# Pooled products, gate sums and convolution steps in a two-block kernel: where they are issued and on which engine

## The chip, the cores and the metric

The kernel runs on one core of one Trainium2 chip. A core has TensorE (matmul), VectorE, ScalarE and GpSimd, each with an in-order queue of its own, and SyncE, whose queue (SP) issues nearly all transfers here. The metric is the time of one execution on the device in microseconds (us).

## The reference

A first block (attention of two kinds, 32 routed experts, a gated embedding) is followed by a second block of two layers, on 256 rows of 1024 columns. The change touches only the second block, which is, cut to what matters:

```python
for l in range(2):
    mod = silu(c) @ w_ada[l] + b_ada[l]
    shift, scale, gate = split(mod, 3)
    h = rms_norm(x, g_pre[l]) * (1 + scale) + shift
    proj = h @ w_in[l]                    # parts 0 to 5, 512 columns each
    u_a, b_a, c_a, gate_a, u_p, gate_p = parts(proj)
    y_a = b_a * causal_conv3(c_a * u_a, w_conv[l]) * silu(gate_a)
    y_p = pool(u_p, w_pool[l]) * pool_scale[l] * silu(gate_p)
    y = concat(y_a, y_p) @ w_out[l]
    x = x + gate * rms_norm(y, g_post[l])
```

`pool` takes, in four groups of 128 columns, the mean of the last 2, 4, 8 or 16 rows less the row itself, and multiplies each group with its own 128 x 128 matrix. All arithmetic is of float32 accuracy.

## The kernel before

Float32 matmuls of large matrices are made of three passes (`mm3`): each operand is split into an upper half (`hi`, rounded) and a residue (`lo`), and hi x hi, hi x lo and lo x hi are summed in PSUM. For every piece of weights ScalarE makes `hi` (L162), and VectorE or GpSimd makes `lo` = raw - hi (L167). A piece is 512 KB: five raw buffers and six hi/lo pairs rotate. PSUM gives three banks to `bulk` (the projections), four to `bank` (transposes, small products) and one to `spare`.

A layer `l` of the second block runs as follows. `normed` (L1084) makes the normalised rows: GpSimd computes the root, VectorE scales (L1094), TensorE transposes (L1024), ScalarE and VectorE apply scale and shift. The parts are then projected by `project` (L1157), each in two halves of 256 columns: a half is 48 matmuls into two `bulk` banks, which the caller empties. First come part 3 and the first half of part 5, by rows (L1137 to L1148), with the weights that `gates_of` has loaded; then, in this order:

- part 4 (`u_p`): ScalarE copies it into PU; GpSimd adds up the windows (L1184), and PW, the pooled features, gets its main part from VectorE (L1187) and its first 16 columns from GpSimd (L1186, L1188).
- part 5, second half: sigmoid on ScalarE, product on VectorE (L1196).
- the four pooled products (L1197 to L1205): TensorE multiplies PW[j] with the pool matrix into a `bank`; ScalarE or VectorE scales it, `gate` transposes and multiplies the gates (j below 2), `split` makes hi and residue (`Yh`, `Yl`).
- part 0 (`u_a`): ScalarE copies it into CU (L1208).
- `ada_acc` for the third part of `mod` (`gate`): silu(c) times 1024 x 1024 weights, 512 columns per call, summed over eight blocks of 128 rows with the partitions kept apart. With GpSimd as its engine each 512 KB load holds four row blocks of 256 columns: two products, then three additions (L581 to L586). With VectorE each load holds two row blocks of 512 columns: two operations (L576, L578). Loads go to the three buffers `adr`, two of which hold weights of the row gates for part of the time; the sums go to the two `acc` buffers, which the gating products `PP` of the block before use first.
- part 2 (`c_a`): VectorE multiplies it into CU (L1214), which empties the bank, and runs the three convolution steps (L1215 to L1217).
- part 1 (`b_a`): VectorE multiplies it into Y (L1219), then `gate` (L1155) and `split`.

After that the partition sums of `gate` are formed on TensorE, and the output projection and the residual close the layer.

The order of the queues is not written out: the program is traced line by line, and a planner simulates the engines and gives each free engine the ready instruction that was traced first. `tc.issue_after(i)` puts those instructions of its block that run on the engine of `i` behind `i`; those on other engines it leaves free. `roots` holds the GpSimd instructions that end each root. The order found is then fixed, and each engine runs its own queue in order.

Of the kernel before, what the change touches and what calls it, by code (L numbers as in the profile page):

```python
# [15 lines left out]
OP = mybir.AluOpType  # L16
AX = mybir.AxisListType.X

S, D, P = 256, 1024, 128
# [78 lines left out]
def block_kernel(ctx: ExitStack, tc: tile.TileContext, a, out, dbg=None, ne=NE):  # L98
    nc = tc.nc
# [6 lines left out]
    def bank():  # L106
        return psum.tile([P, 512], F32, name="bank", tag="bank", bufs=4)

    def bulk():
        return psum.tile([P, 512], F32, name="bulk", tag="bulk", bufs=3)  # L110

    def spare():
        return psum.tile([P, 512], F32, name="spare", tag="spare", bufs=1)

    def slot(tag, n=2048, dt=F32):
        return phase["pool"].tile([P, n], dt, name=tag, tag=tag, bufs=1)
# [16 lines left out]
    def ada_slot(dt=F32):  # L133
        if early.get("adr"):
            return early["adr"].pop(0)
        return phase["pool"].tile([P, 1024], dt, name="adr", tag="adr", bufs=3)

    def mid(shape, dt=F32):
        return work.tile(shape, dt, name="mid", tag="mid", bufs=8)
# [11 lines left out]
    def mm(o, l, r, start, stop):  # L151
        nc.tensor.matmul(o, l, r, start=start, stop=stop)  # L152

    def mm3(o, l, r, start, stop):

        mm(o, l[0], r[0], start, False)
        mm(o, l[0], r[1], False, False)
        mm(o, l[1], r[0], False, stop)

    def split(raw, dst, eng=None):  # L160

        nc.scalar.copy(dst[0], raw)  # L162
        n = raw.shape[-1]
        w = n if eng is None or len(raw.shape) > 2 else min(n, 512)
        for c0 in range(0, n, w):
            cs = slice(c0, min(n, c0 + w))
            (eng or nc.vector).tensor_sub(dst[1][..., cs], raw[..., cs], dst[0][..., cs].bitcast(F32))  # L167
# [38 lines left out]
    def load_split(src, cn, order=None, room=(), eng=None, gains=None, later=None, raws=None):  # L206


        nk = src.shape[0] // P
        kn = min(nk, 1024 // cn)  # L210
        parts, room = {}, dict(room)
        for i in order or range(nk // kn):
            k0 = i * kn
            raw = ((raws or {}).get(i, raw_slot)())[:, :kn * cn]
            nc.sync.dma_start(raw.rearrange("p (k n) -> p k n", k=kn),
                              src[k0 * P:(k0 + kn) * P].rearrange("(k p) n -> p k n", p=P))
            dst = [v[:, :kn * cn] for v in pair(room.get(i))]
            if gains:
                g = vc(gains, i)
                nc.scalar.activation(dst[0], raw, AF.Copy, scale=g)  # L220
                later.append((nc.vector.scalar_tensor_tensor, dst[1], raw, g, dst[0].bitcast(F32), OP.mult, OP.subtract))
            else:
                split(raw, dst, eng[i] if isinstance(eng, list) else eng)
            parts[i] = [v.rearrange("p (k n) -> p k n", k=kn) for v in dst]
        return lambda k, c0, c1: tuple(v[:, k % kn, c0:c1] for v in parts[k // kn])
# [20 lines left out]
    def vc(name, k=0, n=1):  # L246
        return VC[:, VCOL[name] + k:VCOL[name] + k + n]
# [306 lines left out]
    def ada_acc(l, c, e):  # L554

        acc = work.tile([P, 512], F32, name="acc", tag="acc", bufs=2)
        n = 256 if e is nc.gpsimd else 512
        kn = 1024 // n
        for o in range(0, 512, n):
            v = acc[:, o:o + n]  # L560
            for i in range(0, KD, kn):
                w = ada_slot().rearrange("p (k n) -> p k n", k=kn)
                nc.sync.dma_start(w, a["w_ada_2"][l][i * P:(i + kn) * P, c * 512 + o:c * 512 + o + n]
                                  .rearrange("(k p) n -> p k n", p=P))
                if e is nc.scalar:
                    for k in range(2):
                        e.activation(w[:, k], w[:, k], AF.Copy, scale=cact[:, i + k:i + k + 1])
                    if i:
                        nc.gpsimd.tensor_add(w[:, 0], w[:, 0], w[:, 1])
                        nc.gpsimd.tensor_add(v, v, w[:, 0])  # L570
                    else:
                        nc.gpsimd.tensor_add(v, w[:, 0], w[:, 1])
                elif e is nc.vector:
                    for k in range(kn):
                        if i + k == 0:
                            e.tensor_scalar(v, w[:, 0], cact[:, 0:1], None, op0=OP.mult)  # L576
                        else:
                            e.scalar_tensor_tensor(v, w[:, k], cact[:, i + k:i + k + 1], v, op0=OP.mult, op1=OP.add)  # L578
                else:
                    for k in (0, 2):  # L580
                        e.tensor_mul(w[:, k:k + 2], w[:, k:k + 2],  # L581
                                     cact[:, i + k:i + k + 2].unsqueeze(2).to_broadcast([P, 2, n]))
                    e.tensor_add(w[:, 0:2], w[:, 0:2], w[:, 2:4])  # L583
                    e.tensor_add(w[:, 0], w[:, 0], w[:, 1])
                    if i:
                        e.tensor_add(v, first[:, 0], w[:, 0])  # L586
                    first = w
        return acc
# [371 lines left out]
    for e in range(ne):  # L960
# [6 lines left out]
        if e == max(ne - 2, 0):  # L967
            PP = [[perm.tile([P, 512], F32, name="PP", tag=n) for n in ("TA", "TB")],
                  [work.tile([P, 512], F32, name="PP", tag="acc", bufs=2) for _ in range(2)]]
            for t in range(NT):  # L970
                for h in range(2):
                    po = spare()
# [134 lines left out]
    for t in range(NT):  # L1107
# [14 lines left out]
        for h in range(2):  # L1122
            hs, po = slice(h * 512, (h + 1) * 512), pos[h]
# [9 lines left out]
    for l in range(2):  # L1133
# [4 lines left out]
        for t in range(NT):  # L1138
            for dst, ws in ((G[:, t], wgs[:2]), (GP[:, t], wgs[2:])):
                n = 256 * len(ws)  # L1140
                po, sg = bulk()[:, :n], mid([P, n])
# [8 lines left out]
        def gate(dst, g, j):  # L1150

            pt = bank()[:, :S]
            for t in range(NT):
                nc.tensor.transpose(pt[:, t * P:(t + 1) * P], g[:, t, j * P:(j + 1) * P], ident)
            nc.vector.tensor_mul(dst, dst, pt)  # L1155

        def project(part, js=(0, 2), first=None):  # L1157
            for j in js:
                c0 = part * 512 + j * P
                w = first if first and j == js[0] else load_split(wi[:, c0:c0 + 256], 256)  # L1160
                pos = [bulk() for _ in range(2)]
                for k in range(KD):
                    for i in range(2):
                        mm3(pos[i][:, :S], w(k, i * P, (i + 1) * P), (hm[0][:, k], hm[1][:, k]), k == 0, k == KD - 1)
                for i in range(2):
                    yield j + i, pos[i][:, :S]

        def wcv(i, j):
            return vc("w_conv_2", l * 12 + i * 4 + j)

        PUW = wide(s_pu, F32)
        PU = PUW[:, :4 * (16 + S)].rearrange("p (j n) -> p j n", j=4)
# [16 lines left out]
        Y = slot(s_y).rearrange("p (k n) -> p k n", k=KD)  # L1189
# [3 lines left out]
        for j, po in project(5, (2,)):  # L1193
            sgs.append(small([P, S]))
            nc.scalar.activation(sgs[-1], po, AF.Sigmoid)
            nc.vector.tensor_mul(sgs[-1], sgs[-1], po)  # L1196
        for j in range(4):  # L1197
            px, y = bank(), Y[:, 4 + j]
            mm(px[:, :S], wp[:, l, j * P:(j + 1) * P], PW[:, j], True, True)
            if j < 2:  # L1200
                nc.scalar.activation(y, px[:, :S], AF.Copy, scale=vc("pool_scale_2", l * 4 + j))
                gate(y, GP, j)
            else:
                nc.vector.scalar_tensor_tensor(y, px[:, :S], vc("pool_scale_2", l * 4 + j), sgs[j - 2], op0=OP.mult, op1=OP.mult)
            split(y, (Yh[:, 4 + j], Yl[:, 4 + j]))  # L1205
        CU = PU[:, :, 16:]
        for j, po in project(0):
            nc.scalar.copy(CU[:, j], po)  # L1208
        post = slot(s_post).rearrange("p (i n) -> p i n", i=2)
        nc.sync.dma_start(post, a["post"][l:l + 1].to_broadcast([P, 2, D]))  # L1210
        with tc.issue_after(roots[2 * l + 1]):
            accs = [ada_acc(l, 4 + h, nc.gpsimd) for h in range(2)]
        for j, po in project(2):
            nc.vector.tensor_mul(CU[:, j], CU[:, j], po)  # L1214
            nc.vector.tensor_scalar(Y[:, j], CU[:, j], wcv(2, j), None, op0=OP.mult)  # L1215
            nc.vector.scalar_tensor_tensor(Y[:, j, 1:], CU[:, j, :S - 1], wcv(1, j), Y[:, j, 1:], op0=OP.mult, op1=OP.add)
            nc.vector.scalar_tensor_tensor(Y[:, j, 2:], CU[:, j, :S - 2], wcv(0, j), Y[:, j, 2:], op0=OP.mult, op1=OP.add)  # L1217
        for j, po in project(1):
            nc.vector.tensor_mul(Y[:, j], Y[:, j], po)  # L1219
            gate(Y[:, j], G, j)  # L1220
# [77 lines left out]
```

## Time and profile before

| | |
|---|---|
| median of 3 runs | 1435.12 us (1434.74 to 1435.84) |
| profiled execution: time | 1435.64 us |
| profiled execution: span | 1433.8 us |
| mean granted clock of TensorE, share of full speed | 0.974 |
| busy: TensorE | 1306.5 us (91%) |
| busy: VectorE | 626.0 us (44%) |
| busy: ScalarE | 351.6 us (25%) |
| busy: GpSimd | 321.0 us (22%) |

PE stands for TensorE's matmuls, PEld for its weight loads, DVE for VectorE, ACT for ScalarE, POOL for GpSimd, SP for SyncE. The span runs from the first instruction to the last; the time of an execution is somewhat more. A releaser, behind `<-`, is the instruction or transfer that ended an idle time. A granted clock of 1.00 is 2.4 GHz. Layer 0 of the second block lies at about 1213 to 1325 us of the span, with the change's lines from 1225 to 1300; layer 1 follows to the end.

### The profile page before, as it was taken

What the parts mean: (1) busy time and instruction counts of PE and PEld (TensorE: products, weight loads), DVE (VectorE), ACT (ScalarE), POOL (GpSimd) and SP (SyncE); (2) the same over time, 40 slices, a digit from 0 to 9 for tenths busy, and PEclk for the clock granted to TensorE, in tenths of its full rate; (3) what the DMA queues carried; (4) which work ended last, traced back from release to release, by engine and by line L of the source; (5) the groups of instructions that cost most, each with busy time, mean ns of one, the idle gap of its engine ahead of it and who ended that gap; (6) DMA issues with size and microseconds to landing.
All of it is one profiled execution on the core that took longest, in us unless ns stands there. A gap on an engine that the chain in (4) does not pass through costs nothing. (4 is left out here: it accounts for less than half of the span.)

```text
span 1433.8 us, 17081 instructions
## 1 busy us (share of the span) xinstructions
PE 1306.5 (91%) x6831; PEld 706.2 (49%) x6831; DVE 626.0 (44%) x1005; ACT 351.6 (25%) x630; POOL 321.0 (22%) x353
## 2 busy tenths in 40 slices
PE   7989998999999989989989998998999968899987
PEld 6788884333333332333323333333333337887986
DVE  4899963232232221222313233132121248688685
ACT  6756531111111101011100111011111145435432
POOL 5595471000000000000000000000000035785682
PEclk9999997999999999999999999999999979999999
DMA  9739779999999999999999999999999955756651
GB/s 333 245 119 310 253 277 370 428 428 427 426 429 428 428 428 426 428 429 427 428 426 429 426 429 428 427 427 428 427 428 425 423 200 168 235 179 203 215 182 45
DMA packets 100546, 502.44 MB, mean 350 GB/s; under 512 B 7216, under 2 KB 60720, under 8 KB 75632
## 3 DMA queue, kind: packets, MB, share of 16 engines
q1 hardware_dynamic: 99904, 500.59, 86.8%
q8 instruction: 55, 0.90, 0.3%
q10 hardware_dynamic: 560, 0.73, 0.2%
q14 instruction: 27, 0.22, 0.0%
HBM read 500.24 MB, written 1.05 MB: 350 GB/s over the span
## 5 line engine op out<-in xcount | busy, mean ns | idle before, releaser
L152 PE MATMUL bank<-raw,mid 128*64 128x512 f32 x3072 | 692.5, 603 | 43.7 <-DMA raw<-in_w_gate_up_dram 37.6
L152 PEld LDWEIGHTS bank<-raw,mid 128*64 128x64 f32 x3072 | 213.5, 138 | 484.2 <-issue 399.0
L918 POOL CAST BIAS<-BIAS 128x128 fp32r<-128x128 f32 x32 | 10.3, 324 | 827.6 <-PE bank L152 827.5
L854 DVE TENSOR_SCALAR mid<-bank 128x512 f32<-128x512 f32 x32 | 22.1, 692 | 392.8 <-PE bank L152 392.8
L879 DVE SCALAR_TENSOR_TENSOR Y<-bank,ws,Y 64x512 fp32r<-64x512 f32 x64 | 48.0, 750 | 250.3 <-ACT Y L878 250.3
L856 ACT ACTIVATE mid<-mid 128x512 f32<-128x512 f32 x32 | 20.2, 631 | 436.3 <-DVE mid L854 436.3
L167 DVE TENSOR_TENSOR lo<-raw,hi 128x1024 fp32r<-128x1024 f32 (+2 forms) x91 | 116.5, 1301 | 20.4 <-ACT hi L162 20.2
L162 ACT CAST hi<-raw 128x1024 fp32r<-128x1024 f32 (+1 forms) x102 | 105.8, 1041 | 72.4 <-PE bulk L152 55.7
L878 ACT ACTIVATE Y<-bank,ws 64x512 fp32r<-64x512 f32 x64 | 43.7, 682 | 280.2 <-PE bank L152 254.1
L167 POOL TENSOR_TENSOR lo<-raw,hi 128x512 fp32r<-128x512 f32 x50 | 72.8, 1483 | 39.3 <-ACT hi L162 29.9
L152 PE MATMUL bulk<-XS,OH 128*64 128x512 f32 x256 | 63.2, 614 | 4.7 <-DVE X L891 3.2
L152 PE MATMUL bulk<-hi,s 128*128 128x256 f32 (+2 forms) x256 | 59.7, 325 | 8.0 <-ACT hi L162 7.5
L152 PE MATMUL bulk<-s,hi 128*128 128x256 f32 x320 | 62.8, 293 | 0.0
L578 DVE SCALAR_TENSOR_TENSOR acc<-adr,cact,acc 128x512 f32<-128x512 f32 x49 | 54.2, 1105 | 0.6 <-DMA adr<-in_w_ada_dram 0.2
L581 POOL TENSOR_TENSOR adr<-adr,cact 128x512 f32<-128x512 f32 x32 | 45.1, 1434 | 33.5 <-DMA adr<-in_w_ada_dram 33.5
L152 PEld LDWEIGHTS bulk<-s,hi 128*128 128x128 f32 x320 | 51.1, 195 | 0.7 <-DVE s L608 0.2
L152 PEld LDWEIGHTS bulk<-hi,s 128*128 128x128 f32 x256 | 44.2, 196 | 11.7 <-ACT hi L162 7.5
L152 PE MATMUL bulk<-sc,hi 128*128 128x256 f32 x144 | 42.9, 298 | 3.9 <-DVE se L1219 2.1
L152 PE MATMUL bulk<-sa,hi 128*128 128x256 f32 x144 | 42.9, 298 | 3.8 <-DVE sb L1219 2.1
L152 PE MATMUL bulk<-s,lo 128*128 128x256 f32 x160 | 45.9, 291 | 0.0
L891 DVE TENSOR_TENSOR X<-X,bulk 128x512 f32<-128x512 f32 x64 | 42.3, 682 | 1.1 <-PE bulk L152 0.7
L152 PE MATMUL bulk<-lo,s 128*128 128x256 f32 (+2 forms) x128 | 41.7, 327 | 0.9 <-DVE lo L167 0.9
(447 smaller groups left out, 1932.1 us busy)
## 6 DMA issues: line engine op xcount, KB each, us to landing
raw<-in_w_gate_up_dram SPq DMA_DIRECT2D x128, 2048.0 KB, 31.0
raw<-in_w_down_dram SPq DMA_DIRECT2D x64, 2048.0 KB, 34.6
raw<-in_w_in_dram SPq DMA_DIRECT2D x75, 512.0 KB, 4.9
adr<-in_w_ada_dram SPq DMA_DIRECT2D x48, 512.0 KB, 4.5
raw<-in_w_out_dram SPq DMA_DIRECT2D x23, 512.0 KB, 3.6
raw<-in_w_ple_gate_dram SPq DMA_DIRECT2D x5, 512.0 KB, 5.4
raw<-in_w_branch_b_dram SPq DMA_DIRECT2D x4, 512.0 KB, 7.2
raw<-in_w_branch_a_dram SPq DMA_DIRECT2D x4, 512.0 KB, 5.1
```

Of the source, the lines that this page charges most:

```text
L152: nc.tensor.matmul(o, l, r, start=start, stop=stop)
L162: nc.scalar.copy(dst[0], raw)
L167: (eng or nc.vector).tensor_sub(dst[1][..., cs], raw[..., cs], dst[0][..., cs].bitcast(F32))
L578: e.scalar_tensor_tensor(v, w[:, k], cact[:, i + k:i + k + 1], v, op0=OP.mult, op1=OP.add)
L581: e.tensor_mul(w[:, k:k + 2], w[:, k:k + 2], cact[:, i + k:i + k + 2].unsqueeze(2).to_broadcast([P, 2, n]))
L854: nc.vector.tensor_scalar(g_, pG, 7.0, None, op0=OP.min)
L856: nc.scalar.activation(sg, g_, AF.Sigmoid, scale=1.702)
L878: nc.scalar.activation(Y[sl, 0, h], py[sl], AF.Copy, scale=ws[sl, h:h + 1])
L879: nc.vector.scalar_tensor_tensor(Y[sl, 1, h], py[sl], ws[sl, h:h + 1], Y[sl, 0, h].bitcast(F32), op0=OP.mult, op1=OP.subtract)
L891: nc.vector.tensor_add(xv, xv, pc)
L918: nc.gpsimd.tensor_copy(bs, ONE[:, e, :, None].bitcast(F32).to_broadcast([P, 2, SL]))
```

## The change

Three things. The pooled products are traced behind part 0, and `issue_after` puts the matmuls and transposes of products 0 and 1 behind the last matmul of part 0's first half, those of products 2 and 3 behind that of its second half. `ada_acc` of the gates is called with VectorE in place of GpSimd. In part 2 both banks of a half are multiplied into CU before the convolution steps of the half.

```diff
--- before.py
+++ after.py
@@ -1194,7 +1194,13 @@
             sgs.append(small([P, S]))
             nc.scalar.activation(sgs[-1], po, AF.Sigmoid)
             nc.vector.tensor_mul(sgs[-1], sgs[-1], po)
-        for j in range(4):
+        CU, behind = PU[:, :, 16:], []
+        for j, po in project(0):
+            behind.append(nc.cur_bb.bb.instructions[-1])
+            nc.scalar.copy(CU[:, j], po)
+
+        def pooled(j):
+
             px, y = bank(), Y[:, 4 + j]
             mm(px[:, :S], wp[:, l, j * P:(j + 1) * P], PW[:, j], True, True)
             if j < 2:
@@ -1203,18 +1209,22 @@
             else:
                 nc.vector.scalar_tensor_tensor(y, px[:, :S], vc("pool_scale_2", l * 4 + j), sgs[j - 2], op0=OP.mult, op1=OP.mult)
             split(y, (Yh[:, 4 + j], Yl[:, 4 + j]))
-        CU = PU[:, :, 16:]
-        for j, po in project(0):
-            nc.scalar.copy(CU[:, j], po)
+
+        for j in range(4):
+            with tc.issue_after(behind[0 if j < 2 else 2]):
+                pooled(j)
         post = slot(s_post).rearrange("p (i n) -> p i n", i=2)
         nc.sync.dma_start(post, a["post"][l:l + 1].to_broadcast([P, 2, D]))
         with tc.issue_after(roots[2 * l + 1]):
-            accs = [ada_acc(l, 4 + h, nc.gpsimd) for h in range(2)]
-        for j, po in project(2):
-            nc.vector.tensor_mul(CU[:, j], CU[:, j], po)
-            nc.vector.tensor_scalar(Y[:, j], CU[:, j], wcv(2, j), None, op0=OP.mult)
-            nc.vector.scalar_tensor_tensor(Y[:, j, 1:], CU[:, j, :S - 1], wcv(1, j), Y[:, j, 1:], op0=OP.mult, op1=OP.add)
-            nc.vector.scalar_tensor_tensor(Y[:, j, 2:], CU[:, j, :S - 2], wcv(0, j), Y[:, j, 2:], op0=OP.mult, op1=OP.add)
+            accs = [ada_acc(l, 4 + h, nc.vector) for h in range(2)]
+        gen = project(2)
+        for two in zip(gen, gen):
+            for j, po in two:
+                nc.vector.tensor_mul(CU[:, j], CU[:, j], po)
+            for j, _ in two:
+                nc.vector.tensor_scalar(Y[:, j], CU[:, j], wcv(2, j), None, op0=OP.mult)
+                nc.vector.scalar_tensor_tensor(Y[:, j, 1:], CU[:, j, :S - 1], wcv(1, j), Y[:, j, 1:], op0=OP.mult, op1=OP.add)
+                nc.vector.scalar_tensor_tensor(Y[:, j, 2:], CU[:, j, :S - 2], wcv(0, j), Y[:, j, 2:], op0=OP.mult, op1=OP.add)
         for j, po in project(1):
             nc.vector.tensor_mul(Y[:, j], Y[:, j], po)
             gate(Y[:, j], G, j)
```

## Rows read from the trace of the kernel before

**Rows 1.** By stretch: us, busy PE, PEld, DVE, ACT, POOL, clock, DMA share, GB/s.

```profile
1225.30:1242.20 16.90, 16.90 (x144) 16.90 (x143) 9.53 (x9) 7.84 (x13) 16.07 (x16) 1.00 0.63 204
1242.20:1262.80 20.60, 15.69 (x109) 14.74 (x107) 14.86 (x17) 7.70 (x15) 20.42 (x22) 0.92 0.65 211
1262.80:1293.10 30.30, 27.25 (x209) 26.67 (x208) 28.93 (x36) 11.02 (x15) 20.90 (x15) 0.94 0.56 186
```

**Rows 2.** Waits, 1213 to 1325 us: who for whom, total, times, longest.

```profile
ACT hi L162 <- PE bulk L152: 25.3, 13, 5.3
POOL adr L581 <- DMA adr<-in_w_ada_dram: 16.6, 3, 11.3
DVE sa L1187 <- POOL mid L1184: 8.8, 4, 2.8
...
PE bank L152 <- POOL sa L1188: 4.1, 2, 3.0
...
PE bulk L152 <- DVE se L1219: 2.1, 1, 2.1
...
PE bulk L152 <- DVE sa L1214: 0.9, 1, 0.9
...
PE bulk L152 <- DVE small L1196: 0.8, 1, 0.8
```

**Rows 3.** Timeline of TensorE: start, length, ..., idle time before in brackets.

```profile
1244.13 0.70 PE L152 MATMUL bank<-sa,XS 128*128 128x256 f32 x2 [1.13 <-POOL sa L1188]
...
1254.96 0.70 PE L152 MATMUL bank<-sa,XS 128*128 128x256 f32 x2 [2.98 <-POOL sa L1188]
```

**Rows 4.** Busy time in windows of 2 us (columns as in rows 1).

```profile
1256.00:1258.00 2.00, 2.00 (x12) 2.00 (x11) 2.00 (x3) 0.41 (x1) 2.00 (x3) 0.52 0.79 258
1276.00:1278.00 2.00, 1.65 (x13) 1.65 (x14) 1.97 (x6) 0.00 (x0) 0.55 (x1) 1.00 0.58 201
1288.00:1290.00 2.00, 2.00 (x11) 2.00 (x11) 2.00 (x2) 0.70 (x2) 1.93 (x1) 0.50 0.09 23
```

**Rows 5.** Timeline of the VectorE, ahead of the first L1196.

```profile
1245.44 2.06 DVE L167 TENSOR_TENSOR lo<-raw,hi 128x1024 fp32r<-128x1024 f32 x1
1247.42 0.41 DVE L1196 TENSOR_TENSOR small<-small,bulk 128x256 f32<-128x256 f32 x1
```

**Rows 6.** GpSimd's groups, 1213 to 1325 us: busy us, mean ns, idle before.

```profile
L581 POOL TENSOR_TENSOR adr<-adr,cact 128x512 f32<-128x512 f32 x16 | 22.7, 1442 | 16.6 <-DMA adr<-in_w_ada_dram 16.6
```

**Rows 7.** The page's groups of instructions, the accumulation on VectorE.

```profile
L578 DVE SCALAR_TENSOR_TENSOR acc<-adr,cact,acc 128x512 f32<-128x512 f32 x49 | 54.2, 1105 | 0.6 <-DMA adr<-in_w_ada_dram 0.2
```

**Rows 8.** Single lines of the VectorE: duration ns min/median/max, first and last start.

```profile
L578 DVE SCALAR_TENSOR_TENSOR acc<-adr,cact,acc x49: 735/752/1841, 90.6 to 182.5; 128x512 f32<-128x512 f32 x49
...
L1219 DVE TENSOR_TENSOR se<-se,bulk x4: 406/410/414, 1286.3 to 1292.0; 128x256 f32<-128x256 f32 x4
...
L1215 DVE TENSOR_SCALAR se<-sa,VC x4: 343/799/1380, 1270.2 to 1280.9; 128x256 f32<-128x256 f32 x4
```

**Rows 9.** The VectorE's groups, 1213 to 1325 us (columns as in rows 6).

```profile
L167 DVE TENSOR_TENSOR lo<-raw,hi 128x1024 fp32r<-128x1024 f32 x24 | 35.9, 1501 | 7.2 <-ACT hi L162 7.1
L167 DVE TENSOR_TENSOR Yl<-se,Yh 128x256 fp32r<-128x256 f32 x8 | 8.8, 1133 | 0.2 <-ACT Yh L162 0.2
```

**Rows 10.** The same while GpSimd is quiet, 1214 to 1226 us.

```profile
L167 DVE TENSOR_TENSOR lo<-raw,hi 128x1024 fp32r<-128x1024 f32 x5 | 6.0, 1222 | 2.9 <-ACT hi L162 2.8
```

**Rows 11.** Timeline of the VectorE, the L1094 pairs and a split.

```profile
1200.42 0.88 DVE L1094 TENSOR_SCALAR mid<-X,nr 128x512 f32<-128x512 f32 x2 [0.82 <-POOL nr L300]
...
1210.39 2.44 DVE L1094 TENSOR_SCALAR mid<-X,nr 128x512 f32<-128x512 f32 x2 [1.88 <-POOL nr L300]
...
1283.16 2.31 DVE L167 TENSOR_TENSOR lo<-raw,hi 128x1024 fp32r<-128x1024 f32 x1
```

**Rows 12.** Timeline of TensorE, its last wait for L1094.

```profile
1212.98 0.63 PE L1024 MATMUL bank<-cst,mid 128*128 128x128 f32 x4 [0.55 <-DVE mid L1094]
```

**Rows 13.** The page's DMA issues: count, KB each, us to landing.

```profile
raw<-in_w_in_dram SPq DMA_DIRECT2D x75, 512.0 KB, 4.9
```

## The prediction

> **What bounds the kernel now.** I began with the busy shares of the page (table above): TensorE near full, the others under half. That mean hides the stage which the change touches, so busy time by stretch came next, for the last two blocks ("layers" below); each runs the changed lines once [rows 1]. While parts 4 and 5 are projected, TensorE is busy for all 16.90 us; through part 0 and the pooled products for 15.69 of 20.60 us; through parts 2 and 1 for 27.25 of 30.30 us, with the VectorE at 28.93. The stage is TensorE's, with holes. The list of TensorE's waits names them [rows 2]: 4.1 us in two waits for GpSimd's L1188, the last write of a pooled window; 2.1 us for L1219, 0.9 us for L1214, 0.8 us for L1196. The timeline splits the 4.1 us into 1.13 and 2.98 [rows 3]. 1.13 + 0.8 + 2.98 = 4.9 is the idle time of the middle stretch (20.60 - 15.69), and 0.9 + 2.1 = 3.0 that of the third (30.30 - 27.25). The second layer has these five waits again.
>
> A hole costs more than its width. In windows of 2 us the granted clock is 0.52 behind the 2.98 us hole and 0.50 behind the 2.1 us hole, the lower level of 1.2 GHz; behind the 0.9 us hole it stays at 1.00 [rows 4]. As lost time that is (1 - 0.92) x 20.60 = 1.6 us and (1 - 0.94) x 30.30 = 1.8 us [rows 1]. So a layer loses 4.9 + 1.6 + 3.0 + 1.8 = 11.3 us here, two layers 22.6: the most that the stage can give.
>
> **The change, part by part.** The sum is made for one layer, then doubled.
>
> *1. Products behind part 0.* Products 0 and 1 move behind the first half of part 0, products 2 and 3 behind the second. Nothing is added to a queue: the same matmuls, transposes, scalings and splits, and no DMA. Product 2 waited because GpSimd took window sums and accumulation in turns. It moves back by half a part (the first half ran from 1244.8 us to the hole at 1254.96 - 2.98 = 1252.0, wait included [rows 3]), and with GpSimd freed its window is ready well before. Gone are 1.13 + 2.98 + 1.6 of clock = 5.7 us. What is late next is the start of part 0, whose second bank L1196 empties. Until now products 0 and 1 stood ahead of part 0, from 1242.2 to 1244.8 us [rows 1, 3], and covered that eviction; 0.8 us of wait was left, because L1196 ran only at 1247.42, behind a split of 2.06 us [rows 5]. This cover of 2.6 us goes. Against it, a split takes 1.22 us while GpSimd is quiet [rows 10], and the VectorE no longer stands 8.8 us in four waits for window sums [rows 2]. Bounds for the added wait: -0.8 us (all of it goes) and 2.6 us. I take 0.6, nearer the first, since these rows put the lateness on the VectorE and on what GpSimd does to it. Net **5.1 us**.
>
> *2. Accumulation on the VectorE.* It leaves GpSimd: 16 L581 a layer at 1.44 us, and the additions behind them [rows 6]. GpSimd is busy 16 to 21 us in each of the three stretches [rows 1]; window sums, small scalings and some residues remain. To the VectorE come 16 operations of 128x512. The same line runs 49 times there in the attention stage: 735 ns at least, 752 median, 1841 at most, 1105 in the mean [rows 7, 8]. So 16 x 0.75 = 12.0 us at the least, 16 x 1.1 = 17.7 us if GpSimd works beside it as much as there. I take 13, since GpSimd has little left.
>
> Against this stands what the VectorE gets back. Where one operand is in PSUM, its time doesn't change (L1219: 406 to 414 ns); where all are in SBUF, it goes up to several times (L1215: 343 to 1380 ns) [rows 8]. In a layer the splits of weights take 24 x (1.50 - 1.22) = 6.7 us too much, the residues of Y, at the 410 ns of L1219, which has their shape, 8 x (1.13 - 0.41) = 5.8, L1215, by its median, 4 x 0.46 = 1.8 [rows 8 to 10]: 14.3 us together, a little more than comes in. To the third stretch I give half of it: 28.93 - 7.2 = 21.8. Twelve of the added operations find room in the first two stretches, where the VectorE is busy 9.53 of 16.90 and 14.86 of 20.60 us [rows 1]; four more here make 24.8, against 30.30 - 4.8 = 25.5 us that TensorE needs. The VectorE is not the bound, but it has little to spare.
>
> On the path: ahead of L1219 stood a split of 2.31 us [rows 11]; at 1.22 us the eviction comes 1.1 us sooner. The hole of 2.1 us shrinks to 1.0 and then, no wider than the one that left the clock alone, keeps it up: 1.1 + 1.8 = 2.9. The hole of 0.9 us, behind another such split, goes: 3.8 in all. Bounds: 4.8 us if no hole is left; -2.6 us if four added operations at 1.84 us stand in front of evictions. I take off 0.9 us for one added operation and a little, as an average of where the four may stand: **2.9 us**.
>
> At the head of a layer the second pair of L1094 took 2.44 us with GpSimd's first accumulation beside it, the first pair 0.88 us alone, and TensorE stood 0.55 us for it [rows 11, 12]. But the added operations may now start there: the order to stay behind `roots` holds GpSimd's instructions alone. The accumulators take the slots of the last gating products, so none starts before those are used. Bounds 1.6 us and -1.5 us (two operations ahead of a link of the chain); I take **0.5 us**, the row of TensorE's wait.
>
> The Trainium skill (SBUF — State Buffer, "Who interferes with whom") says that a VectorE instruction with two SBUF inputs and a GpSimd instruction that reads SBUF shut each other out, the later one for the whole length of the other. The rows on L1219 and L1215 agree for operands in and out of PSUM. But the rule speaks against the change too: each added operation is of that kind. By it the time would be that of the second rival below.
>
> *3. The new wait.* The VectorE now waits in order for the loads of the gates' weights; behind such a wait stand splits and evictions, and behind those TensorE. GpSimd waited 16.6 us for these loads in a layer, in 3 waits [rows 2]; the VectorE, on the same line in the attention stage, 0.2 us before 49 operations [rows 7]. Bounds 0 and 16.6 us. By the row of the same operation on the same engine I take **-0.6 us**. The eight loads a layer keep their size (512 KB), number and queue (SP's); their rows become twice as long. Taken up sooner, some pass the weights of parts 2 and 1 on SP. That costs nothing while weights lie ready: ScalarE, which makes their upper halves, waited 25.3 us for TensorE to free the buffers [rows 2]. Without that cover one late load is worth its landing, 4.9 us [rows 13].
>
> *4. Evictions ahead of the convolution.* The same four products and twelve steps. In the second pair one eviction moves up; the bank that it frees is not the one awaited in the 0.9 us hole. Nothing of its own; bounds 0.9 and -0.9 us, that hole gone or doubled.
>
> Sum: 5.1 + 2.9 + 0.5 - 0.6 = 7.9 us a layer, 15.8 us in two. The profiled execution took 1435.64 us (span 1433.8, and 1.84 around it), so 1419.8; it lay 0.5 us above the median of the runs, which makes **1419.3 us**.
>
> **The rivals.** *All holes close*: 5.7 + 0.8 + 4.8 + 0.5 = 11.8 a layer, 1435.1 - 23.6 = 1411.5 us. For it: the holes come from late neighbours, not from TensorE's order. Against: three banks leave an eviction little slack. *The VectorE becomes the bound*: the added operations cost 1.1 us and up, and evictions are as late as before: 5.7 - 1.5 - 0.6 = 3.6 a layer, 1427.9 us. For it: 28.93 of 30.30 us. Against: it gets 14.3 us back. *The cover is only moved*: the wait for L1196 grows by all of 2.6 us, and at 3.4 us brings the clock down (1.6): 5.7 - 2.6 - 1.6 - 0.6 = 0.9 a layer, 1433.3 us, which can't be told from no change. Against: the VectorE's own waits just before it go. *Slower: loads hold the VectorE.* If they land later than the order of its queue supposes, GpSimd's 16.6 us a layer stand in front of splits and evictions: 1435.1 - 17.0 + 33.2 = 1451.3 us. It decides once more than 8.5 us a layer get through to TensorE. Against: the attention stage. For: two of the three buffers hold the previous gates' weights until those are used.
>
> **How the numbers follow.** Forecast 0.50, all holes 0.13, VectorE bound 0.20, cover moved 0.08, loads 0.09. The range of 1411 to 1430 us leaves out the last two and a little below, under 2 in 10. A measurement of this kernel can tell about 0.2% (2.9 us) from no change. Within it lies the third rival, less its faster edge: 0.07. Slower is the last rival, 0.09; faster the rest, 0.84.
>
> **What would show it.** Right: TensorE never waits for L1188; the granted clock is 1.00 through part 0; L1215 stays near 0.35 us; the added operations of L578 take about 0.75 us; the list of waits keeps one short wait for L1196 and one for L1219. Wrong: over 2 us of wait for L1196; L578 standing for its load for more than 1 us at a time; the L1094 of a layer's second half later than before; longer waits for L1214 and L1219.

## The result and the profile after

The changed kernel takes 1421.09 us (median; 1417.43 to 1422.69) against 1435.48 us for the kernel before, run beside it: a ratio of 0.990, 95% interval 0.9884 to 0.9916. The forecast was 1419.3 us, with a range of 1411 to 1430. The profiled execution took 1417.43 us (span 1415.6, mean granted clock 0.979), 18.2 us less than that of before.

Not all of this belongs to the change. The first transposes of layer 0 lie ahead of nearly all changed work; they started at 1201.05 us before, and in the timeline of TensorE after they start here (start, length, ..., idle time before in brackets):

```profile
1198.43 1.07 PE L1024 MATMUL bank<-cst,mid 128*128 128x128 f32 x8 [2.22 <-DVE mid L1094]
```

So 2.6 us are a difference of the two executions, and 15.6 us come from the two layers.

In the kernel after, the changed lines have other numbers: the eviction of part 2 is L1223 (was L1214), the convolution steps L1225 to L1227 (L1215 to L1217), the eviction of part 1 L1229 (L1219). What TensorE waits for in the two layers, 1186 to 1416 us (total, times, longest):

```profile
PE bank L1024 <- DVE mid L1094: 9.6, 4, 3.2
PE bulk L152 <- DVE small L1196: 2.7, 1, 2.7
PE bulk L152 <- ACT sc L1038: 1.5, 1, 1.5
PE bulk L152 <- DVE sd L1039: 0.3, 1, 0.3
```

Against [rows 2] there is no wait for L1188 left, and none for either eviction of parts 2 and 1. For the other two, the list of before for the same two layers (1186 to 1434 us) has:

```profile
PE bank L1024 <- DVE mid L1094: 6.1, 6, 1.8
...
PE bulk L152 <- DVE small L1196: 1.6, 2, 0.8
```

So these two waits have grown. By stretch (columns as in [rows 1]) the same is seen:

```profile
1239.30:1260.50 21.20, 18.52 (x136) 18.00 (x135) 15.21 (x19) 10.29 (x18) 9.08 (x10) 0.92 0.55 186
1260.50:1282.40 21.90, 21.90 (x181) 21.73 (x180) 18.52 (x36) 8.91 (x13) 0.00 (x0) 1.00 0.46 150
1295.00:1322.00 27.00, 20.75 (x124) 18.33 (x123) 20.42 (x38) 14.92 (x31) 5.27 (x12) 0.94 0.64 206
...
1344.50:1365.40 20.90, 20.90 (x171) 20.59 (x170) 15.87 (x18) 11.68 (x20) 13.93 (x13) 1.00 0.72 224
```

The second row is parts 2 and 1 of layer 0, but for the start of part 2: TensorE has no hole left, at the full clock, with the VectorE at 18.52 of 21.90 us, where it had 28.93 of 30.30 [rows 1]. The first row is part 0 of layer 0 and that start, with one hole and a clock of 0.92 behind it; the fourth is the same in layer 1, with neither. The third is the head of layer 1, where time was lost; the nearest stretch of before had

```profile
1306.30:1325.30 19.00, 16.11 (x99) 13.83 (x97) 14.27 (x23) 12.01 (x25) 7.23 (x15) 1.00 0.58 191
```

What stands in front of the grown waits is in the VectorE's list of waits for the two layers, and in its timeline ahead of L1094 in layer 1:

```profile
DVE acc L578 <- DMA adr<-in_w_ada_dram: 13.8, 7, 4.2
...
DVE acc L576 <- DMA adr<-in_w_ada_dram: 1.8, 2, 1.3
```

```profile
1300.71 0.75 DVE L578 SCALAR_TENSOR_TENSOR acc<-adr,cact,acc 128x512 f32<-128x512 f32 x1 [1.55 <-DMA adr<-in_w_ada_dram]
1301.38 1.28 DVE L167 TENSOR_TENSOR lo<-raw,hi 128x512 fp32r<-128x512 f32 x2
1302.59 0.88 DVE L1094 TENSOR_SCALAR mid<-X,nr 128x512 f32<-128x512 f32 x2
...
1317.59 0.75 DVE L578 SCALAR_TENSOR_TENSOR acc<-adr,cact,acc 128x512 f32<-128x512 f32 x1 [4.16 <-DMA adr<-in_w_ada_dram]
1318.26 0.87 DVE L1094 TENSOR_SCALAR mid<-X,nr 128x512 f32<-128x512 f32 x2
```

The gate sums start in the head of the layer, in the VectorE's queue ahead of L1094, and wait there for their weights. Three of the seven waits stand shortly ahead of an L1094, with 8.0 of the 13.8 us (1.55 and 4.16 here, 2.27 in layer 0). TensorE's next transposes come late; at these two places of layer 1 it waited 1.56 and 0.71 + 0.61 us before, and now:

```profile
1303.21 1.45 PE L1024 MATMUL bank<-cst,mid 128*128 128x128 f32 x8 [3.08 <-DVE mid L1094]
...
1318.89 1.06 PE L1024 MATMUL bank<-cst,mid 128*128 128x128 f32 x8 [3.18 <-DVE mid L1094]
```

The hole at L1196 in layer 0 has the same sums in front of it, without a wait for a load:

```profile
1239.26 1.12 DVE L578 SCALAR_TENSOR_TENSOR acc<-adr,cact,acc 128x512 f32<-128x512 f32 x1
1240.31 0.42 DVE L1187 SCALAR_TENSOR_TENSOR sa<-mid,sa 128x240 f32<-128x240 f32 x1
1240.65 2.33 DVE L578 SCALAR_TENSOR_TENSOR acc<-adr,cact,acc 128x512 f32<-128x512 f32 x2
1242.91 1.75 DVE L167 TENSOR_TENSOR lo<-raw,hi 128x1024 fp32r<-128x1024 f32 x1
1244.58 0.41 DVE L1196 TENSOR_TENSOR small<-small,bulk 128x256 f32<-128x256 f32 x1
```

### The profile page after: what moved, and what is told of

It is laid out like the page before. It is cut to its first block, busy times and chain, and to the rows that moved or that the text cites. A ratio compares the mean times of both kernels' runs of the same rounds, so it can differ in the third digit from the quotient of the medians.

```text
span 1415.6 us, 17048 instructions
## 1 busy us (share of the span) xinstructions
PE 1298.8 (92%) x6831; PEld 701.6 (50%) x6831; DVE 618.5 (44%) x1037; ACT 351.2 (25%) x630; POOL 238.2 (17%) x281
## 5 line engine op out<-in xcount | busy, mean ns | idle before, releaser
L918 POOL CAST BIAS<-BIAS 128x128 fp32r<-128x128 f32 x32 | 10.2, 322 | 827.2 <-PE bank L152 827.2
L167 DVE TENSOR_TENSOR lo<-raw,hi 128x1024 fp32r<-128x1024 f32 (+2 forms) x91 | 108.8, 1216 | 20.5 <-ACT hi L162 18.8
L578 DVE SCALAR_TENSOR_TENSOR acc<-adr,cact,acc 128x512 f32<-128x512 f32 x77 | 77.7, 1009 | 14.5 <-DMA adr<-in_w_ada_dram 14.0
L152 PE MATMUL bulk<-sc,lo 128*128 128x256 f32 x144 | 41.6, 289 | 0.0
L152 PE MATMUL bulk<-sd,hi 128*128 128x256 f32 x144 | 41.6, 289 | 0.0
```

What stands on the lines that cost most here:

```text
L918: nc.gpsimd.tensor_copy(bs, ONE[:, e, :, None].bitcast(F32).to_broadcast([P, 2, SL]))
```

## The experiments

Theory: the gain comes from freeing GpSimd, and what was lost comes from the places where the VectorE's queue has the gate sums. Rivals: the move of the products makes the larger part, as the prediction's sum has it; or the VectorE's added work itself costs time. The kernel before took 1435.27, 1435.95 and 1435.24 us (medians) beside the three sets of runs. Each edit lets the planner order the queues anew, so a run shows its edit together with the order that it brings.

**One part of the change alone.** First the products: behind part 0 with `issue_after`, as in the change, the rest as before.

```diff
-        for j in range(4):
+        CU, behind = PU[:, :, 16:], []
+        for j, po in project(0):
+            behind.append(nc.cur_bb.bb.instructions[-1])
...
+        for j in range(4):
+            with tc.issue_after(behind[0 if j < 2 else 2]):
+                pooled(j)
...
```

> The kernel before, with only the pooled products moved behind part 0 (GpSimd still accumulates the gates). Theory A, the prediction's: the move itself takes away the waits for the pooled windows, 5.1 us a layer, so about 1425 us, and TensorE's list has no wait for L1188. Theory B: the waits were GpSimd's lateness, and a product moved by half a part meets a window that is still late (the windows of products 2 and 3 ended at 1254.9 and 1261.4 us, the two halves of part 0 would end near 1248 and 1254): the last product still waits some us, and so does L1196, which has lost its cover; 1429 to 1435 us.

Measured: 1430.58 us, ratio 0.9974 (0.9961 to 0.9986), 4.7 us less than before; in the profiled execution the two layers are 2.9 us shorter, and they start 2.3 us sooner. TensorE's waits in the layers (here and below for 1186 to 1440 us):

```profile
PE bank L1024 <- DVE mid L1094: 6.3, 6, 2.1
PE bulk L152 <- DVE small L1196: 5.7, 2, 3.1
PE bulk L152 <- DVE sc L1221: 2.1, 1, 2.1
PE bulk L152 <- DVE sa L1221: 1.9, 1, 1.9
PE bulk L152 <- ACT sc L1200: 1.6, 1, 1.6
...
```

L1188 is gone, as the move promised, but L1196 went from 1.6 to 5.7 us, and an eviction of part 2 (L1221 there) from 1.8 to 4.0. With GpSimd still at work the cover is mostly moved: the prediction's third rival, though not as dear.

Then the engine of the sums:

```diff
-            accs = [ada_acc(l, 4 + h, nc.gpsimd) for h in range(2)]
+            accs = [ada_acc(l, 4 + h, nc.vector) for h in range(2)]
```

> The kernel before, with only the gates accumulated on the VectorE (products and convolution in their old places). Theory A: only the terms of part 2 and 3 of the prediction, 2.8 us a layer, come: about 1429.5 us, with waits of TensorE for pooled windows left. Theory B: the freed GpSimd ends the windows early, the products in their old place wait for nothing and cover L1196 as before; the whole gain comes, 1416 to 1421 us, no worse than the full change, and the one wait for L1196 of 2.7 us in layer 0 shrinks. Both: L578 still waits for its loads ahead of L1094 in the head of the layers.

Measured: 1419.30 us, ratio 0.9892 (0.9877 to 0.9906): the whole gain.

```profile
PE bank L1024 <- DVE mid L1094: 9.1, 4, 5.6
PE bulk L152 <- DVE small L1196: 2.6, 1, 2.6
PE bulk L152 <- ACT sc L1038: 1.5, 1, 1.5
...
```

It has TensorE's waits of the whole change: with the products in their old place no wait for L1188 is left, nor one for L1214 or L1219, and the same two have grown. The shorter wait for L1196 in layer 0 that theory B expected did not come.

Last the evictions:

```diff
-        for j, po in project(2):
...
+        gen = project(2)
+        for two in zip(gen, gen):
+            for j, po in two:
+                nc.vector.tensor_mul(CU[:, j], CU[:, j], po)
+            for j, _ in two:
...
```

> The kernel before, with only both evictions of a half of part 2 ahead of its convolution steps. The prediction: nothing of its own, within 1 us of before (bounds 0.9 us a layer either way), the same five waits of TensorE in each layer. Rival: the eviction order is what closed the holes at L1214 and L1219: 4 us a layer, 1427 us.

Measured: 1435.79 us, ratio 1.0005 (0.9994 to 1.0017): nothing. The same from the other side, the kernel after with part 2 in its old form:

```diff
-        gen = project(2)
-        for two in zip(gen, gen):
...
+        for j, po in project(2):
...
```

> The kernel after, with part 2 in its old form (each eviction with its three steps behind it). By my step 4 the two-by-two evictions are worth nothing: 1419 to 1424 us. If with the gate sums on the VectorE an eviction ahead of the steps matters: 1425 to 1430 us, with TensorE's waits for the eviction of part 2 back at 1 us or more in each layer.

Measured: 1418.88 us, ratio 0.9887 (0.9866 to 0.9907), with 9.7 us of wait for L1094 and 3.1 for L1196 and none for the evictions. Nothing either way.

**The sums held out of the head.** The first sum is put behind the last VectorE instruction of the layer's head, the second behind the second L1196:

```diff
+            emptied = nc.cur_bb.bb.instructions[-1]
...
-        with tc.issue_after(roots[2 * l + 1]):
-            accs = [ada_acc(l, 4 + h, nc.vector) for h in range(2)]
+        accs = []
+        for h, mark in enumerate((halved[2 * l + 1], emptied)):
+            with tc.issue_after(mark):
+                accs.append(ada_acc(l, 4 + h, nc.vector))
```

> The full change, with the first half of the gate sums put behind the last VectorE instruction of the layer's head (the residues of the normalised rows) and the second half behind the second L1196. Theory: what the changed kernel still loses are three waits of L578 for its loads in front of L1094 (TensorE's waits for L1094 sum to 9.6 us in its trace, 6.1 before) and two added operations in front of L1196 in layer 0 (2.7 us of wait and a clock of 1.2 GHz behind it). Fenced, TensorE's waits for L1094 fall by 4 to 5 us over both layers, that for L1196 goes: 6 to 9 us faster than the changed kernel, 1412 to 1415 us. Rival: the added operations only move to other evictions (the head has nothing else to do while it waits for the root), and the time stays at 1420 to 1422 us.

Measured: 1408.13 us, ratio 0.981 (0.9794 to 0.9826). It beats both kernels, and with 13.0 us against the kernel after also the expectation of 6 to 9 us.

```profile
PE bank L1024 <- DVE mid L1094: 3.0, 2, 1.9
PE bulk L152 <- ACT sc L1038: 1.5, 1, 1.5
PE bulk L152 <- DVE sd L1039: 0.3, 1, 0.3
```

The size agrees with the rows. Waits for L1094 and L1196 fall from 9.6 + 2.7 to 3.0, by 9.3 us, of which 0.4 lie ahead of the first transposes of layer 0 (2.22 and 1.86 us); the clock gives back (1 - 0.92) x 21.20 + (1 - 0.94) x 27.00 = 3.3 us (stretches above; here these stretches of both layers run at 1.00): 12.2 us behind those transposes. The span is 9.3 us shorter, and the transposes start at 1201.50 us instead of 1198.43, so inside the layers it is 12.4. The expectation had 4 to 5 us for L1094, where it was 6.6, and nothing for the clock of the head. L578 stands 2.0 us for its loads, in 2 waits, instead of 13.8 in 7.

Which of the two fences does it? Both sums behind the head, none behind L1196:

```diff
-        with tc.issue_after(roots[2 * l + 1]):
+        with tc.issue_after(halved[2 * l + 1]):
```

> The kernel after, with both gate sums ordered behind the last VectorE instruction of the layer's head, and nothing ordered behind L1196. If the head alone makes the gain of accs_fenced (waits of 9.6 us of TensorE for L1094 and the clock behind them): 1408 to 1410 us, with the wait for L1196 of about 2.7 us still there in layer 0 costing under 1 us net. If the added operations ahead of L1196 cost as much as those in the head: 1412 to 1416 us. In both cases TensorE's waits for L1094 come to about 3 us in the two layers and the waits of L578 for its loads to under 5 us.

Measured: 1410.23 us, ratio 0.9819 (0.9804 to 0.9834).

```profile
PE bank L1024 <- DVE mid L1094: 3.1, 2, 2.0
PE bulk L152 <- DVE small L1196: 2.3, 4, 1.0
```

The head makes nearly all of it. The wait for L1196 is spread over four waits of up to 1.0 us; against the kernel with both fences that can't be told from nothing.

**Is the move of the products worth something once the sums stand right?** Both fences, products ahead of part 0 as before:

```diff
-        CU, behind = PU[:, :, 16:], []
...
+        for j in range(4):
             px, y = bank(), Y[:, 4 + j]
...
-        for j in range(4):
-            with tc.issue_after(behind[0 if j < 2 else 2]):
-                pooled(j)
+        CU = PU[:, :, 16:]
...
```

> Like accs_fenced (1408.13 us: the kernel after, with the first gate sums ordered behind the last VectorE instruction of the layer's head and the second behind the second L1196), but the pooled products stand in their old place ahead of part 0. Theory A (with GpSimd freed the place of the products is worth nothing): 1406 to 1411 us, no wait for the window sums' last write, and the wait for L1196 under 1 us. Theory B (the move is worth my predicted 5.1 us a layer): 1418 us, with waits of 1.1 and 3.0 us of TensorE for the window sums in each layer. Theory C (the old place covers the eviction of L1196 better): 1403 to 1406 us.

Measured: 1409.79 us, ratio 0.9811 (0.9798 to 0.9824), beside 0.981 with the move. TensorE's list has two waits for L1188 again, small ones:

```profile
PE bank L152 <- POOL sa L1188: 1.2, 1, 1.2
PE bank L152 <- POOL sc L1188: 0.5, 1, 0.5
```

Of the 8.2 us that L1188 cost before [rows 2], 1.7 are left without any move, and they are too little to show in the time. Theory A holds in the time, not in its word that no wait would be left.

**What the added work costs.** The kernel after without the sums and their loads:

```diff
-            accs = [ada_acc(l, 4 + h, nc.vector) for h in range(2)]
+            accs = []
+            for h in range(2):
+                accs.append(work.tile([P, 512], F32, name="acc", tag="acc", bufs=2))
+                nc.gpsimd.memset(accs[h], 0.0)
```

> The kernel after, with the gate sums left out (a GpSimd memset stands for each; their loads go too). It bounds what the VectorE's added operations, their loads and their places cost. If ordered as in accs_fenced they are hidden: 1403 to 1408 us. If they still take time of TensorE even there: under 1402 us. If the loads of the sums delay nothing but the sums themselves, TensorE's waits in the changed lines are none, and those for L1094 come to 2 to 3 us in the two layers.

Measured: 1407.95 us, ratio 0.9806 (0.979 to 0.9822), as with the sums fenced (1408.13). Thirty-two operations on the VectorE and 8 MB of loads are hidden in full there, as far as the time shows; in the kernel after they cost about 13 us by their place alone. The waits for L1094 came to 4.6 us, where 2 to 3 were expected.

**What GpSimd did to the others.** On the fenced kernel, work that nothing uses, once reading and writing SBUF (the on-chip memory that holds the tiles outside PSUM) and once only writing it:

```diff
+        dum = perm.tile([P, 512], F32, name="dum", tag="TB")
+        with tc.issue_after(roots[2 * l + 1]):
+            nc.gpsimd.memset(dum, 0.0)
+            for _ in range(8):
+                for _ in range(2):
+                    nc.gpsimd.tensor_mul(dum, dum, cact[:, 0:1].to_broadcast([P, 512]))
+                nc.gpsimd.tensor_add(dum, dum, dum)
+                nc.gpsimd.tensor_add(dum[:, :256], dum[:, :256], dum[:, 256:])
```

```diff
...
+            for _ in range(64):
+                nc.gpsimd.memset(dum, 0.0)
```

> accs_fenced, with operations added that nothing uses: GpSimd is kept busy in parts 4 to 2 of each layer by 8 groups of two products and two additions on a scratch buffer in SBUF, close to the gate sums that it had before. If it is GpSimd's reads of SBUF beside VectorE that made VectorE's instructions long and the evictions late: 1416 to 1430 us, L1225 (the first convolution step) well over 0.6 us in the mean, the residues of weights on VectorE near 1.5 us, and TensorE's waits for L1196, L1223 or L1229 back. If it was only that the window sums queued behind the gate sums on GpSimd: TensorE waits for the pooled features or their products, VectorE's steps stay at 0.3 to 0.4 us, and the time is 1410 to 1414 us. If neither matters: 1407 to 1410 us.

> accs_fenced, with 64 GpSimd memsets of 128x512 added per layer in the same place: GpSimd is kept busy but reads nothing in SBUF. By the theory of the reads, VectorE's steps keep their length (L1225 0.3 to 0.4 us) and the time stays at 1407 to 1411 us, unless the window sums queue behind the memsets. If any work of GpSimd makes VectorE's instructions long: as gpsimd_busy_reading, 1414 to 1430 us.

Measured: 1438.77 us with the reads (ratio 1.0022, 1.0012 to 1.0032), 1406.62 us with the writes (0.9801, 0.9785 to 0.9817). With the reads the whole gain is gone: the time lies above the 1416 to 1430 us expected, and 0.2% above the kernel before; the writes cost nothing. Below stand, with the reads, the stretch of 1222 to 1276 us (columns as in [rows 1]) and the VectorE's splits and sums in it (count, busy us, mean ns, idle time before them); then the same with the writes:

```profile
1222.00:1276.00 54.00, 43.63 (x339) 42.51 (x338) 50.75 (x45) 21.93 (x35) 53.17 (x44) 0.93 0.64 214
```

```profile
L167 DVE TENSOR_TENSOR lo<-raw,hi 128x1024 fp32r<-128x1024 f32 x15 | 25.7, 1724 | 0.0
L578 DVE SCALAR_TENSOR_TENSOR acc<-adr,cact,acc 128x512 f32<-128x512 f32 x14 | 17.3, 1234 | 0.1
```

```profile
1222.00:1276.00 54.00, 54.00 (x447) 53.69 (x446) 49.08 (x70) 25.86 (x40) 37.01 (x61) 1.00 0.76 248
```

```profile
L167 DVE TENSOR_TENSOR lo<-raw,hi 128x1024 fp32r<-128x1024 f32 x19 | 24.4, 1282 | 1.1 <-ACT hi L162 1.1
L578 DVE SCALAR_TENSOR_TENSOR acc<-adr,cact,acc 128x512 f32<-128x512 f32 x13 | 11.0, 847 | 2.5 <-DMA adr<-in_w_ada_dram 2.4
```

Without either, GpSimd is busy 18.65 us there, a split takes 1267 ns and a sum 839. So with 37.01 us of mostly writing GpSimd the VectorE's splits and sums stay as they are; 53.17 us of reading GpSimd add 36% to a split and 47% to a sum. GpSimd was busier with the reads; but in 1220 to 1260 us it was busy 39.5 and 37.7 of 40 us in the two, and there a split took 1844 ns with the reads and 1304 with the writes, and TensorE was busy for 33.1 and 40.0 us. Another number of the expectation missed: the first convolution step stayed at 345 ns with the reads, since the added work had ended before the steps began.

The time goes at evictions of the VectorE, by TensorE's list of waits with the reads:

```profile
PE bulk L152 <- DVE small L1196: 12.5, 2, 6.3
PE bank L1024 <- DVE mid L1094: 4.9, 6, 2.2
PE bulk L152 <- DVE sa L1235: 4.2, 1, 4.2
PE bulk L152 <- DVE sc L1235: 4.2, 1, 4.2
```

(L1235 is the eviction of part 2.) In front of L1196 both effects meet. The VectorE stands 2.96 us in its queue for a window sum:

```profile
1250.19 0.83 DVE L1187 SCALAR_TENSOR_TENSOR sa<-mid,sa 128x240 f32<-128x240 f32 x1 [2.96 <-POOL mid L1184]
1250.94 0.41 DVE L1196 TENSOR_TENSOR small<-small,bulk 128x256 f32<-128x256 f32 x1
```

That sum was late on GpSimd, where window sums take up to 1.6 us instead of 0.63 and alternate with the added work, as GpSimd's timeline shows (L1229 to L1231 are added):

```profile
1241.16 1.61 POOL L1184 TENSOR_TENSOR mid<-mid 128x269 f32<-128x269 f32 x1
1242.74 1.48 POOL L1230 TENSOR_TENSOR dum<-dum 128x512 f32<-128x512 f32 x1
...
1244.53 1.61 POOL L1184 TENSOR_TENSOR mid<-sa 128x271 f32<-128x271 f32 x1
1246.11 1.70 POOL L1231 TENSOR_TENSOR dum<-dum 128x256 f32<-128x256 f32 x1
...
1247.95 0.63 POOL L1184 TENSOR_TENSOR mid<-mid 128x269 f32<-128x269 f32 x1
```

The memsets are short (534 ns), so queueing behind long instructions that only write was not tried; how the loss divides between the turns in GpSimd's queue and the length of the instructions stays open. From the second L1196 of layer 0 to its first L1235 (1253 to 1276 us) the VectorE waits for nothing; it works without a gap, with splits of 1.23 to 2.06 us and sums of 1.3 to 1.8. There only the length shows.

## Why the prediction was right, and where it wasn't

The total was right: 15.8 us forecast for the two layers, 15.6 found in them. The terms were not, so that the total is right by luck. By places, in the two layers (forecast, then the waits and clock of the lists above against [rows 1, 2]):

- *Step 1, part 0 and L1196*: +10.2, found +8.6. L1188's 8.2 us and 3.2 of clock are gone. The cover was forecast to cost 0.6 a layer; in layer 0 L1196's wait rose from 0.8 to 2.7 us and took 1.7 of clock with it, in layer 1 it went. The place was right and the cause was not. "Products behind part 0" was to bring this; products_alone brought 4.7 us altogether, and vector_alone brought all without any move. The step counted as the move's what the free GpSimd does: its window sums no longer take turns, so they are ready for the old place as well.
- *Step 2, evictions of parts 2 and 1*: +5.8, found +9.6, the upper bound. Two things were mis-sized. One added operation was put in front of an eviction, but the sums were done before part 2. And of the long instructions ahead of L1219 only the split of 2.31 us was counted; three convolution steps stood there too, of 1.13, 1.14 and 0.94 us, which take 0.34 to 0.48 after. The working on what the VectorE gets back held in part: L1225 takes 343 to 347 ns, the 28 L578 of the layers 751 ns in the median, L1094 478 to 485 (0.88 and 2.44 us for the pairs of [rows 11], 0.88 for both now); but the splits of weights take 1358 ns in the mean of the two layers, against 1518 before and the 1.22 us that the working assumed.
- *Step 2, head of the layer, and step 3, the loads*: +1.0 - 1.2 = -0.2, found -4.7. Waits for L1094 rose from 6.1 to 9.6 us, 0.4 of it ahead of the first transposes of layer 0 and so outside the 15.6 us, with 1.6 us of clock. The two terms are one: what costs is an operation in the head that waits for its load, in front of the chain's next link. It was taken as two small ones, with the load wait of the attention stage, 0.2 us ahead of 49 operations [rows 7]; here it is 13.8 us in 7 waits, 8.0 of it shortly ahead of an L1094. The text had the danger (the order behind `roots` holds GpSimd's instructions alone) and priced it from the wrong row; the cover that it named, the accumulators in use, did not hold the sums back.
- *Step 4*: nothing, and nothing found.

The places sum to 8.6 + 9.6 - 4.7 = 13.5 of 15.6 us; the rest I can't place. So the total came right because an eviction term that was too small and a head term that was too good nearly cancel. Three of the four signs of being wrong that the prediction named came: over 2 us of wait for L1196 (2.7), L578 standing for its load for more than 1 us at a time (up to 4.16), and a later second L1094 (in layer 0 10.6 us behind the first transposes, 9.3 before). Of the rivals, the loads did hold the VectorE, at about 5 us in place of 33; "all holes close" is what accs_fenced reached, with the head mended as well, at 1408.13 against its 1411.5 us.

The rule on two SBUF inputs beside a GpSimd that reads (the Trainium skill, SBUF — State Buffer, "Who interferes with whom") agrees with the two runs on GpSimd: reads lengthen a split from 1267 to 1724 ns, writes to 1282. That one instruction shuts the other out for its whole length these means do not show. The rule's other side, that each added operation would be hit, came to little: seven of the 28 L578 took 1.12 to 1.18 us. The likely reason is that GpSimd has little left to read once the sums are gone: in the first two stretches shown above it is busy for 9.08 and 0.00 us, against 20.42 and 20.90 [rows 1]. L1215, which the prediction read as agreeing with the rule, has one tensor and a column of factors for inputs and is no plain case of it.

## What to carry to other kernels

When work moves to another engine, move its fence too: an order behind an instruction of the old engine doesn't bind the new one, and the work slides forward, here to the front of a chain whose next link it then holds for a load. Price a move by what the engine that is left does to its neighbours, and try that part alone before crediting a reordering. An operation that waits for a load is cheap or dear by what stands behind it in its queue; take the price from the place where it will stand, not from the same line elsewhere.

## Not expected of the hardware

Work of GpSimd whose result nothing uses moved the time by 2.3%: 1438.77 us where it reads SBUF, 1406.62 where it only writes. The reading work was longer in all, but over 40 us in which GpSimd was busy for 39.5 and 37.7 us, a split on the VectorE took 1844 ns beside the reads and 1304 beside the writes; how much of the 2.3% is queueing on GpSimd instead stays open. It works both ways: GpSimd's own window sums took 1.61 us beside the VectorE's splits, and 0.63 us at 1247.95 us, while the VectorE stood idle.
